# Normalising attention probabilities on VectorE in the place of GpSimd: a hybrid Mamba-2 and attention layer in f32 on Trainium2

## The chip, the cores and the metric

One core of one Trainium2 chip runs the whole layer as one launch. The metric is the device time of that launch in microseconds, the median of the runs shown. The text names the engines as the profile does: PE is TensorE's matmuls (PEld its weight loads), DVE is VectorE, ACT is ScalarE, POOL is GpSimd, SP issues the DMAs.

## What is computed

The layer norms its input (adaLN), projects it, feeds two mixers (a Mamba-2 branch and a causal attention with a forget bias), merges them through gates, projects again, adds the residual and norms once more. The change lies in the attention: sequence 1024, 8 heads of 128.

```python
def one_block(args):                      # one block of 128 queries
    qi, fi, pi = args
    logits = jnp.einsum("bhqd,bhkd->bhqk", qi, k).astype(jnp.float32) * scale
    logits = logits + fi[..., :, None] - f_cum[..., None, :]
    logits = jnp.where(pi[:, None] >= kpos[None, :], logits, -jnp.inf)
    probs = jax.nn.softmax(logits, axis=-1).astype(v.dtype)
    return jnp.einsum("bhqk,bhkd->bhqd", probs, v)
...
o = lax.map(one_block, (qb, fq, qpos))
return o * jax.nn.silu(z)
```

Everything is f32. The kernel splits each f32 operand of a product into a high and a low part (names ending in h and l) and sums three matmuls.

## The kernel before

The kernel first projects, then runs the Mamba-2 branch, then the attention (about 728 to 1020 us of the profiled execution), then the merge and the output products. `attend(h, ...)` treats one head. Its 1024 queries are taken as four pairs of 128-query blocks, the longest first (qq = 3, 2, 1, 0); a block b sees n = (b + 1) x 128 keys, so rows have 128 to 1024 columns. For each block:

- L1028, POOL: a triangular mask is put into the forget bias `fb` (128x128).
- L1036, PE: logits into the PSUM tile `lg` (two buffers of 512 columns), three matmuls each.
- L1037, DVE: logits plus bias go to the SBUF tile `pr`, with the row's minimum into `sm` (the logits are negated); L1041, DVE, combines two minima where n is over 512.
- L1042, ACT: the exponential in place, with the row's sum into `sm`; L1044, DVE: its reciprocal.
- L1045, POOL: `pr` times the reciprocal times 0.5, in place. This is the normalisation.

Then for the pair of blocks: L1057, PE, transposes 128x128 pieces of `pr` into the PSUM tile `tp` (two buffers); L1060, ACT, copies them as the high part `pth`, and L1061, DVE, makes the low part `ptl`; L1067, PE, multiplies with v into `pv` (one PSUM buffer); L1070, DVE, multiplies `pv` with the gate `zg`, which also frees `pv` for the next pair.

Other work lies between these steps. The q and k of the next head are projected on PE at L111 to L113 (some are loaded from memory instead), v is loaded for two heads at a time (`v_load`: DMA into `vt`, L98 ACT cast to `vh`, L99 DVE subtraction to `vl`), `u_scaled` (L812 to L815) loads, scales on DVE and stores pieces of the Mamba branch, and behind heads 6 and 7 `early` runs some of the merge's products (L919 to L921, operands `bh` and `bl` made by L98 and L99). `vt`, `ut` and `zg` share one pool of four buffers.

The order within each engine's queue is not the order of the code. The kernel is built with a scheduler that plays through a timeline of its own and appends each instruction to its engine's queue, attention first (`high_priority`); buffers and semaphores follow from it. So an operation that is put on another engine changes the order on all of them from there on. DMAs are issued by SP.

Of the kernel before, what the change touches and what calls it, by code (L numbers as in the profile page):

```python
# [65 lines left out]
def build(ctx, tc, t):  # L66
    nc = tc.nc
    V, A, G, PE, SP = nc.vector, nc.scalar, nc.gpsimd, nc.tensor, nc.sync
# [7 lines left out]
    def f32(ap):  # L76
        return ap.bitcast(F32)
# [559 lines left out]
    with tc.tile_pool(name="sd", bufs=1, side="right") as sd, \  # L637
# [152 lines left out]
        for tb in range(8):  # L790
# [4 lines left out]
                        scalar1=1.0 / 1024, scalar2=4 * EPS, op0=ALU.mult, op1=ALU.add)  # L795
# [184 lines left out]
    with tc.tile_pool(name="at", bufs=1, side="right") as at, \  # L980
# [36 lines left out]
        def attend(h, q, vhl, zg):  # L1017
            qh, ql, kh, kl = q
            vh, vl = vhl
            vs = slice((h % 2) * P, (h % 2 + 1) * P)  # L1020
            fb = at.tile([P, S], F32, tag="fb", bufs=2, name="fb")
            SP.dma_start(out=fb, in_=f_scr[8 * h:8 * h + 8].rearrange("(o c) l -> o (c l)", o=1).broadcast_to([P, S]))
            for qq in (3, 2, 1, 0):
                prs = {}
                for b in (2 * qq + 1, 2 * qq):
                    n = (b + 1) * P
                    bs = slice(b * P, n)
                    G.affine_select(out=fb[:, bs], in_=fb[:, bs], pattern=[[-1, P]], channel_multiplier=1, base=0,  # L1028
                                    compare_op=ALU.is_ge, fill=BIG)
                    pr = at.tile([P, S], F32, tag="pr", bufs=4, name="pr")  # L1030
                    sm = at.tile([P, 2], F32, tag="sm", bufs=4, name="sm")
                    for n0 in range(0, n, 512):
                        n1 = min(n, n0 + 512)
                        lg = atp.tile([P, 512], F32, tag="lg", bufs=2, name="lg")
                        for i, (x, y) in enumerate(((qh, kh), (qh, kl), (ql, kh))):
                            PE.matmul(lg[:, :n1 - n0], lhsT=x[:, bs], rhs=y[:, n0:n1], start=(i == 0), stop=(i == 2))  # L1036
                        V.tensor_tensor_reduce(out=pr[:, n0:n1], in0=lg[:, :n1 - n0], in1=fb[:, n0:n1], op0=ALU.add,  # L1037
                                               op1=ALU.min, scale=1.0, scalar=BIG,
                                               accum_out=sm[:, n0 // 512:n0 // 512 + 1])
                    if n > 512:  # L1040
                        V.tensor_tensor(out=sm[:, 0:1], in0=sm[:, 0:1], in1=sm[:, 1:2], op=ALU.min)  # L1041
                    A.activation(out=pr[:, :n], in_=pr[:, :n], func=AF.Exp, scale=-1.0, bias=sm[:, 0:1],  # L1042
                                 accum_out=sm[:, 1:2])
                    V.reciprocal(out=sm[:, 1:2], in_=sm[:, 1:2])  # L1044
                    G.tensor_scalar(out=pr[:, :n], in0=pr[:, :n], scalar1=sm[:, 1:2], scalar2=0.5,  # L1045
                                    op0=ALU.mult, op1=ALU.mult)
                    prs[b] = pr
                pv = atp.tile([P, 512], F32, tag="pv", bufs=1, name="pv")
                for jp in range(qq + 1):
                    last = jp == qq  # L1050
                    w = 384 if last else 512
                    tp = atp.tile([P, 512], F32, tag="tp", bufs=2, name="tp")
                    blocks = [(2 * jp, 2 * qq, 0), (2 * jp, 2 * qq + 1, 128)]
                    blocks += [(2 * jp + 1, 2 * qq + 1, 256)] if last else [(2 * jp + 1, 2 * qq, 256),
                                                                           (2 * jp + 1, 2 * qq + 1, 384)]
                    for kb, b, o in blocks:
                        PE.transpose(out=tp[:, o:o + P], in_=prs[b][:, kb * P:(kb + 1) * P], identity=ident)  # L1057
                    pth = at.tile([P, 512], F32R, tag="pth", bufs=2, name="pth")
                    ptl = at.tile([P, 512], F32R, tag="ptl", bufs=2, name="ptl")
                    A.copy(out=pth[:, :w], in_=tp[:, :w])  # L1060
                    V.tensor_tensor(out=ptl[:, :w], in0=tp[:, :w], in1=f32(pth[:, :w]), op=ALU.subtract)  # L1061
                    for kb in (2 * jp, 2 * jp + 1):
                        d = (kb % 2) * 256
                        o0 = 128 if (last and kb % 2) else 0
                        m = 256 - o0
                        for i, (x, y) in enumerate(((vh, pth), (vl, pth), (vh, ptl))):
                            PE.matmul(pv[:, o0:256], lhsT=x[kb // 4][:, kb % 4, vs], rhs=y[:, d:d + m],  # L1067
                                      start=(kb == 0 and i == 0), stop=(kb == 2 * qq + 1 and i == 2))
                o = zg[:, qq * 256:(qq + 1) * 256]
                V.tensor_tensor(out=o, in0=pv[:, :256], in1=o, op=ALU.mult)  # L1070
            SP.dma_start(out=o_scr[h], in_=zg[:, :S])
# [6 lines left out]
        for h in range(AH):  # L1078
            if h == HCLOSE:
                hctx.close()  # L1080
                fin = finx.enter_context(tc.tile_pool(name="fin", bufs=1))
            zg = z_load(h)
            with tc.high_priority(offset=APRI):
                attend(h, qkt, vv, zg)
            if h < AH - 1:
                if h % 2:
                    vv = v_load((h + 1) // 2)
                qkt = qk_slab(h + 1)
            if h in EARLY:
                early(EARLY[h])  # L1090
                if 1 in EARLY[h]:
                    ub = b_quads(us_scr, (12, 22))
            for _ in range(PREP[h]):
                u_scaled(next(prep))
# [158 lines left out]
```

## Time and profile before

| | us |
|---|---|
| median of 3 runs | 1218.62 (1217.94 to 1220.36) |
| the profiled execution | 1224.31 |
| its span in the trace | 1222.6 |
| PE busy | 1165.0 (95%) |
| DVE busy | 955.9 (78%) |
| ACT busy | 635.5 (52%) |
| POOL busy | 88.4 (7%) |

The profile is of one execution, whose time stands beside its span: what the trace shows is measured against 1222.6, not against the median. PE's granted clock over the span was 0.988 of full speed. Busy shares are averages over stages; the stage of the change is 292 us long.

### The profile page before, as it was taken

The numbers are of one execution on the slowest core, as the hardware profiler recorded it, in microseconds if no ns is written. First come the engines' busy times: TensorE is split into PE (matmuls) and PEld (weight loads), VectorE is DVE, ScalarE is ACT, GpSimd is POOL, SyncE is SP. The second block draws the span as 40 slices with busy tenths as digits, with TensorE's granted clock in tenths as the row PEclk, the third lists the DMA queues.
The fourth block names the chain that finished last, engine by engine and source line by source line (L and its number), as shares of the span: only waits on it lengthen the run. The fifth ranks groups of instructions, "written<-read, shape, count | busy, mean of one in ns | idle before, by whom it ended". The sixth has DMA issues, their size and how long they took to land.

```text
span 1222.6 us, 18382 instructions
## 1 busy us (share of the span) xinstructions
PE 1165.0 (95%) x6206; PEld 981.2 (80%) x6206; DVE 955.9 (78%) x1946; ACT 635.5 (52%) x1260; POOL 88.4 (7%) x152
## 2 busy tenths in 40 slices
PE   3999999999999999999999989999988999999997
PEld 2788888788877877998887778888877887788876
DVE  5856699788987784589999986664677977989967
ACT  7554443454443334776676633454456554454465
POOL 1000000000000000000000012222322220000001
PEclk9999999999999999999999989999998999999999
DMA  9665643655485676546545668422246526875334
GB/s 370 263 243 166 218 138 100 207 204 176 156 290 171 218 239 201 186 152 222 186 154 178 207 216 286 144 94 81 87 165 203 175 88 228 283 241 181 109 95 147
DMA packets 109018, 228.26 MB, mean 187 GB/s; under 512 B 12362, under 2 KB 20220, under 8 KB 107900
## 3 DMA queue, kind: packets, MB, share of 16 engines
q1 hardware_dynamic: 108924, 227.09, 55.2%
q8 instruction: 49, 0.80, 0.3%
q14 instruction: 45, 0.37, 0.1%
HBM read 159.14 MB, written 67.90 MB: 186 GB/s over the span
## 4 chain that ended last, share of the span: by engine, by line
PE 62%; DVE 16%; DMA 13%; ACT 4%; issue 4%; SPq 1%; POOL 0%; POOLq 0%; DVEq 0%; ACTq 0%
PE pp L497 4%; PE pv L1067 4%; PE pp L499 4%; PE pp L500 4%; PE lg L1036 3%; PE mm L497 3%; PE mm L499 3%; PE mm L500 3%; PE mm L112 3%; PE mm L113 3%; PE mm L111 3%; PE tp L1057 2%; DMA ab<-a_scr 2%; DMA wr<-w_c 2%; PE mm L919 2%
## 5 line engine op out<-in xcount | busy, mean ns | idle before, releaser
L98 ACT CAST wh<-wr 128x512 fp32r<-128x512 f32 (+1 forms) x214 | 131.0, 620 | 176.2 <-DMA wr<-w_c 32.4
L99 DVE TENSOR_TENSOR wl<-wr,wh 128x512 fp32r<-128x512 f32 (+1 forms) x214 | 146.9, 693 | 44.0 <-ACT wh L98 43.3
L112 PE MATMUL mm<-hl,wh 128*128 128x512 f32 x288 | 116.7, 405 | 0.4 <-DVE hl L306 0.4
L111 PE MATMUL mm<-hh,wh 128*128 128x512 f32 x288 | 116.2, 408 | 0.0
L113 PE MATMUL mm<-hh,wl 128*128 128x512 f32 x288 | 115.5, 402 | 0.0
L136 PE MATMUL mm<-wh,hh 128*128 128x256 f32 (+1 forms) x256 | 73.7, 289 | 1.9 <-DVE tmp L348 1.9
L137 PE MATMUL mm<-wl,hh 128*128 128x256 f32 (+1 forms) x256 | 74.4, 291 | 0.0
L138 PE MATMUL mm<-wh,hl 128*128 128x256 f32 (+1 forms) x256 | 73.7, 289 | 0.0
L1042 ACT ACTIVATE pr<-pr,sm 128x1024 f32<-128x1024 f32 (+3 forms) x64 | 49.9, 780 | 42.4 <-DVE sm L1041 35.1
L1060 ACT CAST pth<-tp 128x512 fp32r<-128x512 f32 (+1 forms) x80 | 42.4, 543 | 47.7 <-PE tp L1057 39.5
L1037 DVE CUSTOM_DVE_ANT_0 pr<-lg,fb 128x512 f32<-128x512 f32 (+1 forms) x96 | 51.4, 552 | 17.0 <-PE lg L1036 12.4
L112 PEld LDWEIGHTS mm<-hl,wh 128*128 128x128 f32 x288 | 55.2, 192 | 11.0 <-DVE hl L306 1.0
L113 PEld LDWEIGHTS mm<-hh,wl 128*128 128x128 f32 x288 | 55.0, 191 | 10.4
L111 PEld LDWEIGHTS mm<-hh,wh 128*128 128x128 f32 x288 | 54.7, 193 | 10.2 <-ACT hh L305 0.3
L690 ACT ACTIVATE ab<-ab,acs 128x128 f32<-128x128 f32 x128 | 41.2, 391 | 40.7 <-DMA ab<-a_scr 40.5
L1045 POOL TENSOR_SCALAR pr<-pr,sm 128x1024 f32<-128x1024 f32 (+3 forms) x64 | 51.8, 811 | 87.5 <-DVE sm L1044 70.2
L1061 DVE TENSOR_TENSOR ptl<-tp,pth 128x512 fp32r<-128x512 f32 (+1 forms) x80 | 50.0, 632 | 10.3 <-ACT pth L1060 10.2
L98 ACT CAST sh<-sr 128x512 fp32r<-128x512 f32 x57 | 34.0, 619 | 43.8 <-DVE sr L479 32.4
L796 POOL TENSOR_TENSOR fl<-fl,mhalf 128x8 f32<-128x8 f32 x1 | 1.6, 1647 | 698.2 <-DVE fl L794 698.2
L136 PEld LDWEIGHTS mm<-wh,hh 128*128 128x128 f32 x256 | 48.8, 191 | 2.4 <-DVE tmp L348 2.2
L1067 PE MATMUL pv<-pth,vh 128*128 128x256 f32 (+1 forms) x160 | 45.8, 287 | 4.5 <-DVE zg L1070 3.8
L138 PEld LDWEIGHTS mm<-wh,hl 128*128 128x128 f32 x256 | 49.1, 192 | 0.0
(407 smaller groups left out, 3509.8 us busy)
## 6 DMA issues: line engine op xcount, KB each, us to landing
wr<-w_c SPq DMA_DIRECT2D x116, 256.0 KB, 3.9
wa<-w_ada SPq DMA_DIRECT2D x8, 1024.0 KB, 11.4
g_scr<-gt SPq DMA_DIRECT2D x16, 512.0 KB, 4.2
ab<-a_scr SPq DMA_DIRECT2D x32, 256.0 KB, 3.9
gt<-g_scr SPq DMA_DIRECT2D x32, 256.0 KB, 3.7
wr<-w_ps SPq DMA_DIRECT2D x28, 256.0 KB, 2.6
wr<-w_pa SPq DMA_DIRECT2D x28, 256.0 KB, 2.8
wr<-so SPq DMA_DIRECT2D x28, 256.0 KB, 2.7
```

The lines of the kernel that those rows point to most:

```text
L98: A.copy(out=hi[:, :n], in_=raw[:, :n])
L99: eng.tensor_tensor(out=lo[:, :n], in0=raw[:, :n], in1=f32(hi[:, :n]), op=ALU.subtract)
L111: PE.matmul(ps, lhsT=hi[:, cs], rhs=xh[k][:, hs], start=(k == 0), stop=False)
L112: PE.matmul(ps, lhsT=hi[:, cs], rhs=xl[k][:, hs], start=False, stop=False)
L113: PE.matmul(ps, lhsT=lo[:, cs], rhs=xh[k][:, hs], start=False, stop=(k == 7))
L136: PE.matmul(o, lhsT=xh[k][:, ts], rhs=hi[:, cs], start=(k == 0), stop=False)
L137: PE.matmul(o, lhsT=xh[k][:, ts], rhs=lo[:, cs], start=False, stop=False)
L138: PE.matmul(o, lhsT=xl[k][:, ts], rhs=hi[:, cs], start=False, stop=(k == 7))
L497: PE.matmul(ps, lhsT=f[0][:, w], rhs=xh[:, hs], start=(first and k == 0), stop=False, skip_group_check=True)
L499: PE.matmul(ps, lhsT=f[0][:, w], rhs=xl[:, hs], start=False, stop=False, skip_group_check=True)
L500: PE.matmul(ps, lhsT=f[1][:, w], rhs=xh[:, hs], start=False, stop=(k == 3), skip_group_check=True)
L1067: PE.matmul(pv[:, o0:256], lhsT=x[kb // 4][:, kb % 4, vs], rhs=y[:, d:d + m], start=(kb == 0 and i == 0), stop=(kb == 2 * qq + 1 and i == 2))
```

## The change

One line: the normalisation L1045 is issued on VectorE instead of GpSimd, with the same operands.

```diff
@@ -1042,7 +1042,7 @@
                     A.activation(out=pr[:, :n], in_=pr[:, :n], func=AF.Exp, scale=-1.0, bias=sm[:, 0:1],
                                  accum_out=sm[:, 1:2])
                     V.reciprocal(out=sm[:, 1:2], in_=sm[:, 1:2])
-                    G.tensor_scalar(out=pr[:, :n], in0=pr[:, :n], scalar1=sm[:, 1:2], scalar2=0.5,
+                    V.tensor_scalar(out=pr[:, :n], in0=pr[:, :n], scalar1=sm[:, 1:2], scalar2=0.5,
                                     op0=ALU.mult, op1=ALU.mult)
                     prs[b] = pr
```

These are 64 instructions (8 heads of 8 blocks). All other instructions stay; the scheduler sets the queues of PE, DVE and ACT anew from the first head on. Three places of the order:

Head 0, ACT, while the values of the next pair of heads are loaded; before:

```order
L1060 CAST pth<-tp 128x384
L1042 ACTIVATE pr,sm<-pr,sm 128x512
L98 CAST vh<-vt 128x1024
L1042 ACTIVATE pr,sm<-pr,sm 128x384
L1060 CAST pth<-tp 128x512 x2
```

and with the change:

```order
L1060 CAST pth<-tp 128x384
L98 CAST vh<-vt 128x1024
L1042 ACTIVATE pr,sm<-pr,sm 128x512
L1042 ACTIVATE pr,sm<-pr,sm 128x384
L1060 CAST pth<-tp 128x512 x2
```

The cast of `vh`, which waits for a DMA, has moved ahead of the exponential of 512 columns. The same place on DVE, before:

```order
L1037 ISA pr,sm<-lg,fb 128x384
L1037 ISA sm 128x1
L1044 RECIPROCAL sm<-sm 128x1
L99 TENSOR_TENSOR vl<-vt,vh 128x1024
L1044 RECIPROCAL sm<-sm 128x1
L1070 TENSOR_TENSOR zg<-pv,zg 128x256
L1061 TENSOR_TENSOR ptl<-tp,pth 128x512 x2
```

and with the change:

```order
L1037 ISA pr,sm<-lg,fb 128x384
L1037 ISA sm 128x1
L99 TENSOR_TENSOR vl<-vt,vh 128x1024
L1044 RECIPROCAL sm<-sm 128x1 x2
L1045 TENSOR_SCALAR pr<-pr,sm 128x512
L1045 TENSOR_SCALAR pr<-pr,sm 128x384
L1061 TENSOR_TENSOR ptl<-tp,pth 128x512
L1070 TENSOR_TENSOR zg<-pv,zg 128x256
L1037 ISA pr,sm<-lg,fb 128x256
```

Both normalisations and one `ptl` now stand ahead of `zg`, and `vl` ahead of both reciprocals.

Head 6, DVE, where `early` forms its operands; before:

```order
L99 TENSOR_TENSOR bl<-wr,bh 128x512
L1070 TENSOR_TENSOR zg<-pv,zg 128x256
L99 TENSOR_TENSOR bl<-wr,bh 128x512
L1041 TENSOR_TENSOR sm<-sm 128x1
L1037 ISA pr,sm<-lg,fb 128x512
L1037 ISA sm 128x1
L1037 ISA pr,sm<-lg,fb 128x128
L1037 ISA sm 128x1
```

and with the change:

```order
L99 TENSOR_TENSOR bl<-wr,bh 128x512
L1045 TENSOR_SCALAR pr<-pr,sm 128x1024
L1070 TENSOR_TENSOR zg<-pv,zg 128x256
L99 TENSOR_TENSOR bl<-wr,bh 128x512
L1041 TENSOR_TENSOR sm<-sm 128x1
L1037 ISA pr,sm<-lg,fb 128x512
L1037 ISA sm 128x1
L1044 RECIPROCAL sm<-sm 128x1
L1037 ISA pr,sm<-lg,fb 128x128
L1037 ISA sm 128x1
```

A normalisation of 1024 columns stands between the first `bl` and `zg`, and a reciprocal before the last eviction.

Head 7, DVE, the last long blocks; before:

```order
L1044 RECIPROCAL sm<-sm 128x1
L1041 TENSOR_TENSOR sm<-sm 128x1
L1037 ISA pr,sm<-lg,fb 128x512
L1037 ISA sm 128x1
L1037 ISA pr,sm<-lg,fb 128x128
L1037 ISA sm 128x1
L1044 RECIPROCAL sm<-sm 128x1
L1041 TENSOR_TENSOR sm<-sm 128x1
L1044 RECIPROCAL sm<-sm 128x1
```

and with the change:

```order
L1041 TENSOR_TENSOR sm<-sm 128x1
L1037 ISA pr,sm<-lg,fb 128x512
L1037 ISA sm 128x1
L1044 RECIPROCAL sm<-sm 128x1
L1037 ISA pr,sm<-lg,fb 128x128
L1037 ISA sm 128x1
L1045 TENSOR_SCALAR pr<-pr,sm 128x896
L1041 TENSOR_TENSOR sm<-sm 128x1
L1044 RECIPROCAL sm<-sm 128x1
L1045 TENSOR_SCALAR pr<-pr,sm 128x768
```

The reciprocal of the 896-column block has moved behind the eviction of 512 columns, and its normalisation behind that of 128. PE at the same place, as a difference (minus is before, plus with the change):

```order
 L1036 MATMUL lg<-kh,ql 128x128
-L1057 MATMUL tp<-ident,pr 128x128 x8
 L1036 MATMUL lg<-kh,qh 128x512
 L1036 MATMUL lg<-kl,qh 128x512
 L1036 MATMUL lg<-kh,ql 128x512
 L1036 MATMUL lg<-kh,qh 128x384
 L1036 MATMUL lg<-kl,qh 128x384
 L1036 MATMUL lg<-kh,ql 128x384
+L1057 MATMUL tp<-ident,pr 128x128 x8
 L1067 MATMUL pv<-pth,vh 128x256
```

The eight transposes of the first pair have moved behind six logit matmuls of the next.

## Rows read from the trace of the kernel before

**Rows 1.** The page: busy us of each engine (share of the span) and instructions, and the shares of the chain that ended last.
```profile
PE 1165.0 (95%) x6206; PEld 981.2 (80%) x6206; DVE 955.9 (78%) x1946; ACT 635.5 (52%) x1260; POOL 88.4 (7%) x152
...
PE 62%; DVE 16%; DMA 13%; ACT 4%; issue 4%; SPq 1%; POOL 0%; POOLq 0%; DVEq 0%; ACTq 0%
```

**Rows 2.** Windows: the attention stage and its dense middle; columns: stretch, us, then busy us (instructions) of PE, PEld, DVE, ACT and POOL, granted PE clock, DMA share, GB/s.
```profile
728.00:1020.00 292.00, 279.90 (x1599) 242.78 (x1600) 200.50 (x513) 145.57 (x294) 76.31 (x128) 0.97 0.44 145
775.00:900.00 125.00, 123.84 (x755) 109.50 (x754) 76.89 (x221) 60.49 (x124) 35.28 (x63) 1.00 0.30 101
```

**Rows 3.** PE's waits in 728 to 1020 us: us in total, times, longest us.
```profile
PE lg L1036 <- DVE sm L1037: 5.0, 5, 3.2
PE pv L1067 <- DVE zg L1070: 3.8, 4, 2.2
PE lg L1036 <- DMA fb<-f_scr: 1.5, 1, 1.5
...
PE tp L1057 <- POOL pr L1045: 0.5, 1, 0.5
```

**Rows 4.** The page's costliest groups: the normalisation; busy us, mean ns of one, idle us before it.
```profile
L1045 POOL TENSOR_SCALAR pr<-pr,sm 128x1024 f32<-128x1024 f32 (+3 forms) x64 | 51.8, 811 | 87.5 <-DVE sm L1044 70.2
```

**Rows 5.** Timeline of the tail, all engines (start us, us, engine, line, operation, out<-in, count, and in brackets the idle time before it and what ended it).
```profile
1000.95 1.00 POOL L1045 TENSOR_SCALAR pr<-pr,sm 128x896 f32<-128x896 f32 x1
...
1002.00 1.09 PE L1057 MATMUL tp<-ident,pr 128*128 128x128 f32 x8 [0.46 <-POOL pr L1045]
...
1010.37 1.48 DVE L1061 TENSOR_TENSOR ptl<-tp,pth 128x512 fp32r<-128x512 f32 x2
...
1011.10 0.19 PEld L1067 LDWEIGHTS pv<-ptl,vh 128*128 128x128 f32 x1 [0.24 <-DVE ptl L1061]
```

**Rows 6.** Timeline, all engines, at two places where a normalisation runs beside DVE.
```profile
739.52 2.61 POOL L1045 TENSOR_SCALAR pr<-pr,sm 128x1024 f32<-128x1024 f32 x1 [6.27 <-DVE sm L1044]
...
739.92 1.28 DVE L813 SCALAR_TENSOR_TENSOR ut<-ut,cols,rb 128x1024 f32<-128x1024 f32 x1
...
913.18 1.12 POOL L1045 TENSOR_SCALAR pr<-pr,sm 128x1024 f32<-128x1024 f32 x1 [0.89 <-DVE sm L1044]
...
913.52 0.78 DVE L1041 TENSOR_TENSOR sm<-sm 128x1 f32<-128x1 f32 x1
```

**Rows 7.** Groups of DVE by shape: three of the whole span, and L813 in 728 to 1020 us: busy us, mean ns of one | idle us before.
```profile
L543 DVE TENSOR_SCALAR cv<-xp,cols 128x1024 f32<-128x1024 f32 x10 | 7.7, 808 | 0.2 <-ACT xp L539 0.2
...
L285 DVE TENSOR_SCALAR acc<-wa,cols 128x256 f32<-128x256 f32 x8 | 2.8, 347 | 1.1 <-DMA wa<-w_ada 1.1
...
L560 DVE TENSOR_SCALAR gb<-wga,cols 128x1024 f32<-128x1024 f32 x1 | 0.8, 758 | 0.0
...
L813 DVE SCALAR_TENSOR_TENSOR ut<-ut,cols,rb 128x1024 f32<-128x1024 f32 x8 | 10.2, 1284 | 10.2 <-DMA ut<-u_scr 6.6 <-DMA rb<-r_scr 3.6
```

**Rows 8.** Timeline of ACT, head 0.
```profile
762.10 0.72 ACT L1042 ACTIVATE pr<-pr,sm 128x512 f32<-128x512 f32 x1 [0.98 <-DVE sm L1037]
...
764.08 1.04 ACT L98 CAST vh<-vt 128x1024 fp32r<-128x1024 f32 x1 [1.17 <-DMA vt<-v_scr]
765.03 0.61 ACT L1042 ACTIVATE pr<-pr,sm 128x384 f32<-128x384 f32 x1
```

**Rows 9.** Timeline of DVE, head 0.
```profile
765.16 1.23 DVE L99 TENSOR_TENSOR vl<-vt,vh 128x1024 fp32r<-128x1024 f32 x1 [2.05 <-ACT vh L98]
766.30 0.15 DVE L1044 RECIPROCAL sm<-sm 128x1 f32<-128x1 f32 x1
766.38 0.41 DVE L1070 TENSOR_TENSOR zg<-pv,zg 128x256 f32<-128x256 f32 x1
766.70 1.28 DVE L1061 TENSOR_TENSOR ptl<-tp,pth 128x512 fp32r<-128x512 f32 x2
```

**Rows 10.** Timeline of PE, head 0.
```profile
766.93 0.36 PE L1067 MATMUL pv<-pth,vh 128*128 128x256 f32 x1 [2.23 <-DVE zg L1070]
```

**Rows 11.** Windows behind the two longest gaps of PE in the stage (columns as in rows 2).
```profile
767.70:771.00 3.30, 3.30 (x18) 3.30 (x17) 1.90 (x5) 0.88 (x1) 0.29 (x1) 0.50 0.37 144
771.10:775.00 3.90, 3.90 (x19) 3.17 (x19) 3.19 (x8) 2.56 (x8) 1.05 (x2) 1.00 0.39 99
...
918.50:924.60 6.10, 6.10 (x21) 5.23 (x22) 4.46 (x12) 4.96 (x10) 3.25 (x4) 0.50 0.90 311
```

**Rows 12.** Timeline at head 6, all engines.
```profile
914.97 0.62 ACT L98 CAST bh<-wr 128x512 fp32r<-128x512 f32 x1 [3.43 <-DMA wr<-us_scr]
914.98 0.28 PE L1036 MATMUL lg<-kh,ql 128*128 128x128 f32 x1
915.62 0.69 DVE L99 TENSOR_TENSOR bl<-wr,bh 128x512 fp32r<-128x512 f32 x1 [0.97 <-ACT bh L98]
916.23 0.42 DVE L1070 TENSOR_TENSOR zg<-pv,zg 128x256 f32<-128x256 f32 x1
...
916.99 0.69 DVE L99 TENSOR_TENSOR bl<-wr,bh 128x512 fp32r<-128x512 f32 x1 [0.34 <-ACT bh L98]
917.59 0.15 DVE L1041 TENSOR_TENSOR sm<-sm 128x1 f32<-128x1 f32 x1
917.66 0.69 DVE L1037 CUSTOM_DVE_ANT_0 pr<-lg,fb 128x512 f32<-128x512 f32 x1
...
918.41 0.80 PE L1036 MATMUL lg<-kh,qh 128*128 128x512 f32 x1 [3.15 <-DVE sm L1037]
```


## Prediction

> **What bounds the kernel now.** I read the busy line of the page first: PE is busy 95% of the span, DVE 78%, ACT 52%, POOL 7%, and the chain that ended last lies on PE for 62% and on POOL for 0% [rows 1]. TensorE sets the time. The change touches only the attention, so next comes that stage alone, 728 to 1020 us: PE is busy 279.9 of 292.0 us, so it idles 12.1; DVE is busy 200.5, POOL 76.3 [rows 2]. What PE waits for there is the next view: 5.0 us for DVE to evict logits, 3.8 for DVE's zg, 1.5 for a DMA, and 0.5, once, for the normalised probabilities of POOL [rows 3]. The reader is to see that GpSimd's lateness costs 0.5 us and VectorE's close to 9: the change moves work off an engine that nobody waits for, onto the one that PE waits for most. In the dense middle, 775 to 900, PE loses only 1.2 of 125 us and DVE has 48 us free [rows 2]. What happens is therefore decided at a few places.
>
> **What is removed.** POOL's 64 normalisations, 51.8 us busy [rows 4]. PE's one wait for them stands at 1002.00 [rows 5]. The PE queue after the change puts six lg matmuls ahead of these transposes, and their buffer is freed by an eviction that ends near 1002, so the idle time there hardly goes. I take -0.3, bounds 0 and -0.5.
>
> The normalisation itself gets shorter: an undisturbed 1024-column one takes 1.12 us on POOL [rows 6] and, by the price below, 0.76 on DVE; over all 64 that is 51.8 against 33.2, or 18.6 us of latency. By the waits only 0.5 of it is latency that PE sees. The Trainium skill (GPSIMD Engine Reference, section 4.1, Engine selection) says that elementwise work on a tile belongs on VectorE, GpSimd being roughly at line rate with one input and about 2x slower with two. By the rows and the price the factor is 1.5. By the rule the sum would be a gain, up to 18.6 us if all of that latency counted, and by the waits no more than 0.5 us.
>
> **What is added.** 64 TENSOR_SCALARs of 128 to 1024 columns on DVE, eight of each size. The trace has no such operation with a per-partition pointer and a constant. The nearest rows are f32 TENSOR_SCALARs from SBUF to SBUF: 758 ns at 1024 columns, 347 at 256, and 808 for a form with two pointers [rows 7]. The line through the first two is 210 ns + 0.535 per column: 0.76, 0.69, 0.62, 0.55, 0.48, 0.42, 0.35, 0.28 from 1024 down to 128, together 4.15 us a head and 33.2 for eight heads. With the 50 ns of a second pointer it is 36.4; at the price of a two-tensor operation (1284 ns at 1024 [rows 7]), 33.2 x 1.69 = 56. I take 33.2 to 36, since the operation has one tensor. DVE in the stage goes from 69% to 81% and still has 56 us free, so the sum of the work decides nothing. What hides it are DVE's gaps, in which it waits for ACT's exponentials and PE's logits, and PE's filler (the next head's q and k products). Where the order puts a normalisation directly ahead of something that PE takes at once, the cover is gone and its whole length is paid.
>
> **Place A, head 0, the largest term.** Before, the exponential of 512 columns runs on ACT at 762.10, and only then ACT waits, 1.17 us, for the load of v: vh runs at 764.08, the exponential of 384 at 765.03 [rows 8]. DVE's vl starts at 765.16, the second reciprocal at 766.30, zg at 766.38 [rows 9], and PE, idle 2.23 us, starts pv at 766.93 [rows 10]. After, the vh cast stands ahead of both exponentials, and DVE has vl, two reciprocals, two normalisations (512, 384), one ptl and only then zg. My working, with the trace's durations: vh to 765.13, the exponentials (pipelined steps of 0.72 and 0.61) to 766.46; vl to 766.39, reciprocals to 766.7, normalisations +0.48 +0.42, to 767.6; ptl (0.64, half of the two at 766.70 [rows 9]) to 768.2; zg to 768.5; pv at about 768.6, +1.7. Three transposes that came behind the pv now run inside the wait, -0.3 (eight take 1.09 us [rows 5]). **+1.4**; bounds +0.3 (the load lands early or ACT is ready sooner) and +1.7.
>
> The gap also touches the clock. After the idle 2.23 us, PE ran at a granted clock of 0.5 from 767.7 to 771.0, 3.3 us, and at 1.0 again from 771.1; after the idle 3.15 us before 918.41 it ran at 0.5 for 6.1 us, to 924.6 [rows 11, 12]. Those are the 1.2 and the 2.4 GHz level. The new gap is 3.6 to 3.9 us with three transposes in it, so nearer to the second. Another 3 us or so at half speed costs 1.5 to 1.7: bounds 0 and +1.7, taken **+1.2**.
>
> **Place B, head 6.** PE stands from 915.26 to 918.41 because its next lg waits for the eviction at 917.66, behind bl, zg, bl and a combine of minima on DVE [rows 12]. After, a 1024-column normalisation stands between the first bl and zg: 0.76 more. DVE had 0.34 idle before the second bl [rows 12], which absorbs that much: **+0.4**, bounds 0 and 0.76.
>
> **The tail, head 7, without filler.** The 896-column normalisation now stands behind the evictions of 512 and 128 columns. It ends about 1003.1 instead of 1001.95 [rows 5]; that is 1.15 later, and the six lg matmuls moved ahead cover most of it: +0.3. At 1010.37 ptl is started as soon as zg is done and PE waits for it until 1011.10 [rows 5]; a 384-column normalisation now stands ahead: +0.4. The last transposes moved behind a pv: +0.2. Together **+0.9**, bounds 0 and 1.5.
>
> **Elsewhere.** In six other places of heads 1, 3, 4 and 5 a normalisation stands directly ahead of a zg, ptl or eviction that PE uses soon: three of 512, one each of 640, 384 and 1024 columns, 3.2 us by the price. The order of PE's queue has been redone around them, and the dense stretch loses only 1.2 in 125 us now [rows 2], so I take under a third, **+0.9**, bounds 0 and 3.2.
>
> **Sum:** -0.3 + 1.4 + 1.2 + 0.4 + 0.9 + 0.9 = **+4.5 us**. It is made against the profiled execution (1224.31 us, span 1222.6), which ran 5.7 above the median; the stage's waits should be the same in the others, so the sum is put on the median, 1218.62: **1223.1 us**. About 0.2%, 2.4 us, is what a measurement of this kernel tells from no change: the three runs shown spread by 2.4. The sum of the bounds is -0.2 to +8.9.
>
> **Rivals.**
> - *Hidden.* All of it falls in DVE's gaps. For: 56 us still free, dense stretch without PE waits. Against: places A, B and the tail are exactly where DVE is last. It needs the load at A to land by about 762, before the exponentials are ready; then A and its clock fall away (-2.6) and the rest, +1.9, is below what can be told: 1220.5.
> - *Faster.* POOL and DVE hold each other now: a 1024-column normalisation took 2.61 us at 739.52 while L813 ran beside it, and a one-element combine took 0.78 at 913.52, under a normalisation, instead of the 0.15 at 917.59 [rows 6, 12]. Without POOL reading, DVE's results come earlier. If that closes the 3.15 us gap before 918.41, it and half of the 6.1 us at half clock go, -6.2; with the other terms at half (+2) the time is 1214.4. It decides if the first bl, at 915.62 now, can start some 3 us earlier. Against: after the held combine DVE waits 0.97 us for ACT's bh cast at 914.97 anyway [rows 12], so the lead is thrown away there. The Trainium skill (SBUF — State Buffer, Who interferes with whom) says that GpSimd shares DVE's second port pair, and that a DVE instruction with two SBUF inputs and a GpSimd one that reads SBUF block each other, whichever starts first winning; the trace agrees at both rows.
> - *Slower by much.* The operation costs nearer 1284 ns at 1024 (56 us in all, DVE at 88%), all places pay in full (8.9) and two or three gaps more grow long enough to draw a stretch at half clock of 3.3 us each, 1.65 lost: +12, 1230.6. For: PE takes many DVE results at once. Against: the price rows.
>
> **How the numbers follow.** Forecast (+2.4 to +8) 0.43; much slower (+8 to +13) 0.12; hidden (within 2.4) 0.28; faster (-2.4 to -7) 0.17. So slower 0.55, same 0.28, faster 0.17. The range leaves out the lower half of the faster case (0.08) and the upper part of the slow one (0.06): 1214 to 1230; that of the forecast by itself is 1221 to 1226.6.
>
> **What would show it.** Right: L1045 on DVE at about 0.76 us for 1024 columns and 33 to 36 us in all; DVE near 235 us in the stage; PE's wait for zg at head 0 up from 2.2 to over 3.5, with a half-clock stretch of 5 to 7 us behind it; the gap of 3.15 slightly longer. The stage then lasts some 4 us more, and what follows it as long as before. Wrong: the vt load landing earlier, the vh cast off ACT's path, the gap at head 6 gone, or L1045 above 1 us at 1024 columns, each of which would move the sum by more than its own term, since a gap takes its half-clock stretch with it.

## The result, and the profile after

The changed kernel takes 1225.62 us (median of 5 runs, 1223.99 to 1226.98) against 1220.19 for the kernel before (5 runs): the ratio is 1.0044, 95% interval 1.0027 to 1.0060, 5.4 us slower. The forecast was 1223.1, 4.5 us slower than the 1218.62 it started from.

The two profiled executions do not show this in their spans, 1222.3 us after and 1222.6 before: the profiled execution of before (1224.31) ran 4 us above its median, that of after (1223.99) 1.6 below. So the spans say nothing here, and the reading goes place by place (times in a trace are microseconds from the start of its own span). The page of after, busy time of each engine and the shares of the chain (compare [rows 1]):

```profile
PE 1163.0 (95%) x6206; PEld 979.3 (80%) x6206; DVE 981.6 (80%) x2010; ACT 634.4 (52%) x1260; POOL 38.3 (3%) x88
...
PE 64%; DVE 13%; DMA 13%; ACT 4%; issue 4%; SPq 1%; POOL 0%; DVEq 0%; POOLq 0%; ACTq 0%
```

POOL has lost 50 us, DVE has gained 25.7, and the chain still lies on PE. The attention stage, in the columns of [rows 2]:

```profile
728.00:1020.00 292.00, 277.56 (x1594) 240.69 (x1592) 225.00 (x576) 144.03 (x293) 25.52 (x63) 0.98 0.43 144
...
775.00:900.00 125.00, 123.82 (x754) 109.56 (x753) 90.43 (x250) 61.04 (x125) 12.95 (x31) 1.00 0.28 95
```

DVE goes from 200.5 to 225.0 us, less than the 33 added; the dense middle loses 1.2 us of PE in both kernels. PE's waits in the stage, in the form of [rows 3]:

```profile
PE lg L1036 <- DVE sm L1037: 4.9, 6, 2.7
PE tp L1057 <- DVE ptl L1061: 3.1, 1, 3.1
PE pv L1067 <- DVE zg L1070: 3.1, 2, 2.7
PE pv L1067 <- DVE ptl L1061: 1.0, 4, 0.4
...
PE pv L1067 <- DVE sm L1044: 0.7, 1, 0.7
```

The wait for POOL is gone, and all that is shown here is for DVE (left out: 0.9 for ACT's pth). A new kind stands second: transposes that wait 3.1 us for a ptl. That is head 0 (PE's and DVE's timeline, and ACT's behind it):

```profile
766.20 0.55 PE L1057 MATMUL tp<-ident,pr 128*128 128x128 f32 x3 [3.09 <-DVE ptl L1061]
766.62 0.36 PE L1067 MATMUL pv<-pth,vh 128*128 128x256 f32 x1
```
```profile
764.50 0.34 DVE L1044 RECIPROCAL sm<-sm 128x1 f32<-128x1 f32 x2
764.75 0.80 DVE L1045 TENSOR_SCALAR pr<-pr,sm 128x512 f32<-128x512 f32 x2
765.46 0.68 DVE L1061 TENSOR_TENSOR ptl<-tp,pth 128x512 fp32r<-128x512 f32 x1
766.06 0.41 DVE L1070 TENSOR_TENSOR zg<-pv,zg 128x256 f32<-128x256 f32 x1
```
```profile
762.28 1.05 ACT L98 CAST vh<-vt 128x1024 fp32r<-128x1024 f32 x1 [2.67 <-DMA vt<-v_scr]
763.23 0.72 ACT L1042 ACTIVATE pr<-pr,sm 128x512 f32<-128x512 f32 x1
...
763.95 0.60 ACT L1042 ACTIVATE pr<-pr,sm 128x384 f32<-128x384 f32 x1
```

The vh cast runs first, both exponentials behind it, and DVE does two reciprocals, two normalisations (0.80 us for the two) and a ptl before zg, as the order said. PE idles 3.09 us, against 2.23 in [rows 10]. From the start of the vh cast to the end of PE's wait it is 3.92 us here (762.28 to 766.20) and 2.85 before (764.08 [rows 8] to 766.93 [rows 10]); the experiments come back to these two numbers.

The normalisation on DVE, by size, the combine of minima and the low parts of early's operands, in groups of the stage (busy us, mean ns of one):

```profile
L99 DVE TENSOR_TENSOR bl<-wr,bh 128x512 fp32r<-128x512 f32 x16 | 10.7, 686 | 1.7 <-ACT bh L98 1.6
...
L1045 DVE TENSOR_SCALAR pr<-pr,sm 128x1024 f32<-128x1024 f32 x8 | 6.0, 752 | 0.2
...
L1041 DVE TENSOR_TENSOR sm<-sm 128x1 f32<-128x1 f32 x32 | 4.9, 152 | 0.2
...
L1045 DVE TENSOR_SCALAR pr<-pr,sm 128x128 f32<-128x128 f32 x8 | 2.3, 283 | 0.1
```
```profile
L1045 DVE TENSOR_SCALAR pr<-pr,sm 128x1024 f32<-128x1024 f32 (+3 forms) x64 | 33.0, 520 | 1.2
```

752 ns at 1024 columns and 283 at 128: the line through [rows 7] gave 758 and 278, and 33.2 us in all. The combine L1041 fell from a mean of 215 ns, the row of before,

```profile
L1041 DVE TENSOR_TENSOR sm<-sm 128x1 f32<-128x1 f32 x32 | 6.9, 215 | 0.1
```

to 152, with no normalisation on POOL beside it any more.

Two further places. The first is the zg of head 5 (DVE, then PE, then the same pv before, which waited 0.59 us):

```profile
932.97 0.48 DVE L1045 TENSOR_SCALAR pr<-pr,sm 128x512 f32<-128x512 f32 x1
...
933.44 0.67 DVE L954 TENSOR_TENSOR wr<-b,wr 128x512 f32<-128x512 f32 x1
934.03 0.42 DVE L1070 TENSOR_TENSOR zg<-pv,zg 128x256 f32<-128x256 f32 x1
```
```profile
934.59 0.55 PE L1067 MATMUL pv<-pth,vh 128*128 128x256 f32 x1 [2.66 <-DVE zg L1070]
```
```profile
935.41 0.36 PE L1067 MATMUL pv<-pth,vh 128*128 128x256 f32 x1 [0.59 <-DVE zg L1070]
```

The second is the place that the prediction calls head 6 (its order is that of early's operands, which stand behind head 6 in the code). By the count of zg it lies between head 4's last block and head 5's first. Its normalisation is there, and the gap is 2.74 us where [rows 12] has 3.15:

```profile
914.57 0.75 DVE L1045 TENSOR_SCALAR pr<-pr,sm 128x1024 f32<-128x1024 f32 x1
...
915.73 0.69 DVE L99 TENSOR_TENSOR bl<-wr,bh 128x512 fp32r<-128x512 f32 x1
...
917.16 0.58 PE L1036 MATMUL lg<-kh,qh 128*128 128x512 f32 x1 [2.74 <-DVE sm L1037]
```

The granted clock behind the gap at head 0, and behind that at 934 (columns as in [rows 2]):

```profile
767.20:770.60 3.40, 3.40 (x16) 3.11 (x15) 3.16 (x8) 2.37 (x6) 0.28 (x1) 0.51 0.40 141
770.70:775.00 4.30, 4.30 (x22) 3.52 (x21) 2.42 (x7) 1.21 (x2) 0.30 (x1) 1.00 0.52 155
...
934.60:937.90 3.30, 3.30 (x15) 3.27 (x16) 3.30 (x6) 0.47 (x1) 0.00 (x0) 0.50 0.00 0
```

Both stretches run at 0.5, the 1.2 GHz level, for about 3.4 us; the first is no longer than that of [rows 11], the second is new.

### The profile page after: what moved, and what is told of

It is laid out like the page before. It is cut to its first block, busy times and chain, and to the rows that moved or that the text cites. A ratio compares the mean times of both kernels' runs of the same rounds, so it can differ in the third digit from the quotient of the medians.

```text
span 1222.3 us, 18276 instructions
## 1 busy us (share of the span) xinstructions
PE 1163.0 (95%) x6206; PEld 979.3 (80%) x6206; DVE 981.6 (80%) x2010; ACT 634.4 (52%) x1260; POOL 38.3 (3%) x88
## 4 chain that ended last, share of the span: by engine, by line
PE 64%; DVE 13%; DMA 13%; ACT 4%; issue 4%; SPq 1%; POOL 0%; DVEq 0%; POOLq 0%; ACTq 0%
PE pp L497 4%; PE pp L499 4%; PE pp L500 4%; PE pv L1067 4%; PE mm L112 3%; PE mm L113 3%; PE mm L497 3%; PE mm L111 3%; PE mm L499 3%; PE mm L500 3%; PE lg L1036 3%; DMA ab<-a_scr 2%; PE tp L1057 2%; PE mm L136 1%; PE mm L137 1%
## 5 line engine op out<-in xcount | busy, mean ns | idle before, releaser
L112 PEld LDWEIGHTS mm<-hl,wh 128*128 128x128 f32 x288 | 55.0, 191 | 11.1 <-DVE hl L306 1.0
L1067 PE MATMUL pv<-ptl,vh 128*128 128x256 f32 (+1 forms) x160 | 48.3, 302 | 1.2 <-DVE ptl L1061 1.0
L137 PEld LDWEIGHTS mm<-wl,hh 128*128 128x128 f32 x256 | 48.9, 191 | 0.2
```

Of the source, the lines that this page charges most:

```text
L112: PE.matmul(ps, lhsT=hi[:, cs], rhs=xl[k][:, hs], start=False, stop=False)
L137: PE.matmul(o, lhsT=xh[k][:, ts], rhs=lo[:, cs], start=False, stop=False)
```

## Experiments

**Again, to know what belongs to one execution.** The kernel before and the changed one, unchanged, traced a second and the changed one a third time.

> The kernel before, unchanged, for a second trace of it. It tells which of the traced differences are the program's and which belong to one execution. Few places: the gaps of PE at head 0 (2.23 us), before 918.41 (3.15) and the small ones near 935 (0.59, 0.27, 0.81) come again within 0.3 us. Clock by chance: the stretches at half clock (6.8, 3.4 and 6.8 us long behind 727, 767 and 918) differ in length from one execution to the next, by whole steps of 3.4 us.

> The changed kernel, unchanged, timed once more and traced a second time. Few places: 5 us over before again (0.3 to 0.6%), with the gaps of 3.09 us at head 0 and 2.66 us at 934.6 both there, the second with a stretch at half clock behind it. Clock by chance: the two gaps stay but the stretch at 934 may be missing or twice as long, and the difference to before moves by 1.7 us per step of 3.4 us.

> The changed kernel, unchanged, a third time, beside the two that follow. If the whole is what the first two comparisons gave, 5 to 6 us over before. If the parts by head are right and the whole was read too high by chance, about 2 us over before. In the trace: gap at head 0 over 3 us, gap of 2.4 to 2.7 us near 934, both with a stretch at half clock.

The two further comparisons gave 1.0049 [1.0033, 1.0066] and 1.0040 [1.0020, 1.0060]: the whole is 5 to 6 us, three times. The gaps are the program's, but not to 0.3 us. Kernel before, second trace (PE, head 0 and the place behind head 4):

```profile
772.68 0.36 PE L1067 MATMUL pv<-pth,vh 128*128 128x256 f32 x1 [2.63 <-DVE zg L1070]
```
```profile
924.91 0.80 PE L1036 MATMUL lg<-kh,qh 128*128 128x512 f32 x1 [3.97 <-DVE sm L1037]
```

2.23 became 2.63, 3.15 became 3.97. The stretches at half clock behind 727, 767 and 918 came again with the lengths of the first trace; one of 3.4 us at 1020, which the first trace has, did not. Changed kernel, second and third trace, head 0:

```profile
770.67 0.33 PE L1057 MATMUL tp<-ident,pr 128*128 128x128 f32 x1 [3.36 <-DVE ptl L1061]
```
```profile
764.45 0.47 PE L1057 MATMUL tp<-ident,pr 128*128 128x128 f32 x1 [3.51 <-DVE ptl L1061]
```

The gap at 934 was 2.66, 2.38 and 1.65 us in the three traces, the last less than expected, and half clock followed each. The granted clock, which every timed run lists as a mean, is lower with the change in both comparisons that list it for both kernels: 0.9887 (6 runs) against 0.9909 (17), and 0.9855 (12) against 0.9892 (29). One minus the clock, times the span, is the time that PE loses to it: 13.9 against 11.1 us, and 17.8 against 13.2. So 2.8 us of 6.0 come with the clock in the first comparison, 4.6 of 4.9 in the second, and the rest without.

**The change undone for a head or two.**

```diff
-                    V.tensor_scalar(out=pr[:, :n], in0=pr[:, :n], scalar1=sm[:, 1:2], scalar2=0.5,
+                    (G if h == 0 else V).tensor_scalar(out=pr[:, :n], in0=pr[:, :n], scalar1=sm[:, 1:2], scalar2=0.5,
```

and `h in (4, 5)` in the second.

> The change undone for head 0 alone: its 8 normalisations on POOL, the other 56 on DVE. Few places: the gap at head 0 falls from 3.09 us to the 2.2 of before and the rest stays, so 4 us over before (1.3 less than the changed kernel). Spread evenly over the heads: one eighth of 5.4 us comes back, 4.7 us over before. In the trace the exponential of 512 columns stands ahead of the vh cast again.

> The change undone for heads 4 and 5: 16 normalisations on POOL, 48 on DVE. Few places: the gap of 2.66 us at 934.6 shrinks to the 0.6 of before and its stretch at half clock (1.7 us) goes, 3.8 us less than the changed kernel, so 1.6 us over before (0.13%). Spread evenly over the heads: a quarter of 5.4 us comes back, 4 us over before.

Measured: 1.0042 [1.0026, 1.0059] and 1.0035 [1.0019, 1.0051] over before, beside 1.0049 for the changed kernel on the same chip: 5.1 and 4.3 us. For the first, 4 and 4.7 both lie in the interval; for the second (2.3 to 6.2 us) the 1.6 of few places does not, the 4 of an even spread does. The gaps did what was expected. PE at head 0 in the first, and another wait that had not been foreseen, 11 us earlier:

```profile
768.98 0.36 PE L1067 MATMUL pv<-pth,vh 128*128 128x256 f32 x1 [2.02 <-DVE zg L1070]
```
```profile
757.83 0.39 PE L1067 MATMUL pv<-ptl,vh 128*128 128x256 f32 x1 [1.08 <-DVE ptl L1061]
```

and PE at head 5 in the second:

```profile
935.30 0.36 PE L1067 MATMUL pv<-pth,vh 128*128 128x256 f32 x1 [0.67 <-DVE zg L1070]
```

0.67 instead of 2.66, and no half clock there; yet the time fell by 1.7 us only, which the intervals do not tell from nothing. The account by place below says why: what the gap at 934 costs had come back at the place before it.

**One group of heads on DVE alone.** The condition is turned round (`V if h == 0 else G`, then heads 1 to 3, 4 and 5, 6 and 7). From the end of such a group on the order is that of before.

> Only head 0 normalised on DVE, heads 1 to 7 on POOL; from head 1 on the order is that of before. Few places: the gap of head 0 is the 3.1 to 3.4 us of the changed kernel, 1.3 us lost, and the stretch at half clock behind it comes in more executions than before, another 0 to 1.7: 1.3 to 3 us over before. Spread evenly: 0.7 us.

> Only heads 1 to 3 on DVE, where the normalisation has the filler of the next head's q and k beside it. Few places: no gap of PE over 0.3 us beside those of before, within 1 us of before. Spread evenly: three eighths of 5.4, 2 us over before.

> Only heads 4 and 5 on DVE. Few places: the gap of 2.4 to 2.7 us before the pv near 934 with its stretch at half clock, 2.1 + 1.7 = 3.8 us over before. Spread evenly: 1.4 us.

> Only heads 6 and 7 on DVE, the tail among them. Few places: the tail's gaps of the changed kernel, 0.7 us more idle than before, so 0 to 1 us over before. Spread evenly: 1.4 us. The four runs of this set add up to the change if the parts do not touch each other: 5.4 us.

| on DVE | ratio to before | 95% interval |
|---|---|---|
| head 0 | 1.0010 | 0.9995 to 1.0025 |
| heads 1 to 3 | 0.9994 | 0.9976 to 1.0012 |
| heads 4, 5 | 1.0003 | 0.9982 to 1.0024 |
| heads 6, 7 | 1.0009 | 0.9989 to 1.0029 |

Together 0.16%, 2 us, with an interval of some 4.5 us to either side (the root of the summed squares of the four half widths, times 1220): this neither adds up to the change nor contradicts it. 3.8 us for heads 4 and 5 is outside (0.24% is 2.9), and so are the 2 us of an even spread for heads 1 to 3 (0.12% is 1.5). By time alone no group stands out. In the trace of heads 4 and 5 the expected gap near 934 did not come: that pv waits 0.9 us for zg and no half clock follows, so heads 4 and 5 by themselves do not make the gap of 1.65 to 2.66 us there.

**What the traces say, place by place.** With the groups there are eleven traces that share PE instructions. Head 0 first: in six of them head 0 has the order of before, in five that of the change. PE's gap before the pv (or, with the change, before the transposes ahead of it), and whether a stretch of half clock of about 3.4 us follows:

| head 0 as before | gap, us | half clock | head 0 as changed | gap, us | half clock |
|---|---|---|---|---|---|
| before | 2.23 | yes | changed | 3.09 | yes |
| before, second | 2.63 | yes | changed, second | 3.36 | yes |
| heads 1 to 3 | 2.40 | yes | changed, third | 3.51 | yes |
| head 0 undone | 2.02 | no | heads 4, 5 undone | 3.62 | yes |
| heads 6, 7 | 2.73 | no | head 0 alone | 3.67 | yes |
| heads 4, 5 | 0.38 | no | | | |

The row with the smallest and one with the largest gap:

```profile
766.18 0.36 PE L1067 MATMUL pv<-pth,vh 128*128 128x256 f32 x1 [0.38 <-ACT pth L1060]
```
```profile
770.12 0.33 PE L1057 MATMUL tp<-ident,pr 128*128 128x128 f32 x1 [3.67 <-DVE ptl L1061]
```

And the clock over the 3.5 us from the end of the gap on, in heads 6, 7 (full) and in head 0 alone (half):

```profile
765.80:769.30 3.50, 3.42 (x23) 3.11 (x24) 2.63 (x6) 1.14 (x3) 0.63 (x2) 1.00 0.52 150
```
```profile
770.50:774.00 3.50, 3.50 (x15) 3.20 (x14) 3.40 (x9) 2.42 (x6) 0.29 (x1) 0.51 0.36 110
```

The means are 2.07 and 3.45 us, and the half clock comes in 3 of 6 and in 5 of 5. (With eight such stretches in eleven traces, all five would fall on the changed order by chance about once in eight times.)

How long PE waits depends on when the load of v lands. ACT waits for it in all eleven traces, also in that with 0.38 us:

```profile
763.34 1.05 ACT L98 CAST vh<-vt 128x1024 fp32r<-128x1024 f32 x1 [1.42 <-DMA vt<-v_scr]
```

There the cast starts 0.74 us earlier than in the first trace of before and PE comes to the place 1.1 us later, so before the change the place could also cost next to nothing. What does not scatter is the chain behind the load. From the start of the vh cast to the end of PE's wait it takes 2.84 or 2.85 us in each of the six traces with the order of before, and 3.92 or 3.93 in each of the five with that of the change. The order adds 1.08 us, every time; the rest of the difference between the two means is the load's.

To see what arrives on the path, I took the start of the same PE instructions in a trace and in the first trace of before, and how the difference grows across a stretch in which both have the same work to do (first the traces of the unchanged programs, then those of the variants):

| stretch | traces with its order changed | traces with its order of before |
|---|---|---|
| head 0 (736 to 800) | +1.5, +1.8, +0.8, +0.8, +2.4 | 0, +0.4, +0.1, +0.2, -0.2, -3.4 |
| heads 1 to 3 (800 to 900) | +0.3, +0.2, +0.2, +0.5, +0.3, +0.4 | 0, +0.1, 0, -0.2, +0.1 |
| heads 4, 5 (900 to 970) | +0.2, +0.1, +1.3, +0.4, +1.0 | 0, +0.4, -0.3, +0.1, -0.2, -0.7 |
| heads 6, 7 (970 to 1027) | +1.4, +1.4, +1.3, +1.4, +1.1, +1.1 | 0, +0.2, 0, +0.2, 0 |

The last line leaves out a stretch of half clock at 1020 (3.4 us, 1.7 lost) where only one of the two has it. By the difference of the means the change costs 1.9 us at head 0 (1.4 without the trace with the 0.38 us gap), 0.3 at heads 1 to 3, 0.7 at heads 4 and 5, 1.2 in the tail: 4.1 in all. That the gap at 934 weighs little is seen in the third line: every trace with the order of before has half clock for over 6 us behind the gap near 918, two of the three of the changed kernel for 3.4, and another 3.4 behind 934.

**The load of v taken out of the way.** In both kernels the scaling of the Mamba pieces is spread, so that the load for heads 2 and 3 is not queued behind their buffers at head 0.

```diff
-PREP = (6, 1, 0, 0, 0, 0, 0, 0, 1)
+PREP = (2, 1, 2, 2, 0, 0, 0, 0, 1)
```

> The changed kernel with the scaling of the Mamba pieces spread: PREP = (2, 1, 2, 2, ...) in the place of (6, 1, 0, 0, ...), so four pieces that were scaled in head 0 come in heads 2 and 3, and the load of v for heads 2 and 3 no longer waits behind their stores. Few places: the gap at head 0 (3.1 to 3.4 us with a stretch at half clock) goes to under 0.5, 4 us or more less than the changed kernel, so about before or a little under. Spread evenly: only the DMA wait goes, with the same gain in both kernels, 2.2 to 3.9 us.

> The same spreading in the kernel before. Few places: the gap of 2.2 to 2.6 us at head 0 and its stretch at half clock go, 2 to 4 us less than before; the normalisation on DVE then costs only what the place near 934 costs, so spread_u_dve is 2.5 to 4 us slower than this one. Spread evenly: spread_u_dve is 5.4 us slower than this one, as with the wait.

Measured: 0.9985 [0.9968, 1.0002] with the normalisation on DVE, 0.9983 [0.9963, 1.0002] with it on POOL. Neither can be told from before, and between the two lie 0.02%, 0.2 us, with some 3 us of uncertainty. PE has no gap at head 0 in either trace (ACT still waits 2.7 and 3.3 us for a load of v, at 746 and 748, while PE has other work). PE's waits, first with DVE, then with POOL:

```profile
PE lg L1036 <- DVE sm L1037: 6.1, 5, 3.9
PE tp L1057 <- DVE ptl L1061: 1.6, 1, 1.6
PE pv L1067 <- DVE zg L1070: 1.3, 3, 0.6
...
PE tp L1057 <- DVE pr L1045: 0.3, 1, 0.3
```
```profile
PE lg L1036 <- DVE sm L1037: 6.0, 6, 3.6
PE pv L1067 <- DVE zg L1070: 1.5, 3, 0.6
...
PE tp L1057 <- POOL pr L1045: 0.5, 1, 0.5
```

The 5.4 us of an even spread lie outside; of the 2.5 to 4 of few places only the lower end is inside. With DVE the transposes near 931 still wait 1.6 us for a ptl, without half clock behind them. The scheduler sets another order in the tail too, and from 900 to 1045 both traces gain the same against before, 2.1 us. The mean granted clock is 0.9905 with DVE and 0.9904 with POOL, so the change takes nothing from the clock here. The 33 us on DVE stayed and cost nothing that can be told, so the loss is no price of DVE's time as such: it hangs on the wait for v and on the order that the scheduler makes around it. Which of these two it is more was not parted, since the edit changes both.

**POOL's free time used.** The low parts of the early products, made on POOL.

```diff
-                fs.append(b_split(e))
+                fs.append(b_split(e, G))
```

> spread_u_dve with the low parts bl of the early products (20 subtractions of 128x512) made on POOL, which the change has left idle, in the place of DVE. Few places: at the two places of heads 4 and 5 DVE no longer stands behind bl's wait for a DMA, so the gap of 3.2 us before the lg near 918 and that of 2.7 near 934 shrink, with their half clock: 3 to 8 us less than spread_u_dve, and under before. Against: POOL's masks of the forget bias stand behind bl in its queue and the gap stays, 0.

Measured: 1214.75 us (median of 6) against 1221.5 (of 29), a ratio of 0.9930 [0.9904, 0.9957]: 8.5 us faster than before by the ratio, 6.8 by the medians, and the fastest kernel here. (There are twelve such subtractions, not twenty.) PE's wait for evictions, the subtraction on POOL, and the window behind 914.8 us (columns as in [rows 2]):

```profile
PE lg L1036 <- DVE sm L1037: 4.1, 7, 0.9
```
```profile
L99 POOL TENSOR_TENSOR bl<-wr,bh 128x512 fp32r<-128x512 f32 x12 | 16.0, 1354 | 6.4 <-ACT bh L98 5.3 <-DMA wr<-us_scr 0.9
```
```profile
914.80:918.00 3.20, 3.20 (x12) 2.64 (x13) 1.02 (x8) 2.84 (x6) 1.65 (x3) 0.50 1.04 407
```

The longest wait falls from 3.9 us to 0.9, although a subtraction takes 1354 ns on POOL against 686 on DVE: DVE's queue no longer stands behind operands that a DMA brings late. From 900 to 1027 us this trace gains 6.2 us on that of the variant it starts from. The half clock that was expected to go with the gap stayed: 3.4 us, as in the other two traces with the scaling spread, here behind waits of 0.28, 0.56 and 0.86 us. It was not run in the kernel before, with POOL also normalising.

## Why the prediction was right

**The bound and the removed wait.** Right. The one wait for POOL (0.46 us at 1002.00 [rows 5]) is now a wait of the same length for an eviction, the one that the prediction named:

```profile
1001.45 0.50 PE L1036 MATMUL lg<-kh,qh 128*128 128x512 f32 x1 [0.46 <-DVE sm L1037]
...
1001.59 0.68 DVE L1045 TENSOR_SCALAR pr<-pr,sm 128x896 f32<-128x896 f32 x1
...
1002.78 1.04 PE L1057 MATMUL tp<-ident,pr 128*128 128x128 f32 x8
```

so the gain was 0, not 0.3.

**The price.** Right: 33.0 us in all against 33.2 to 36. DVE's busy time in the stage is 225 us and not 235. The forecast added durations, and busy time counts a moment once, while records of consecutive DVE instructions overlap: the normalisations of 764.75 start before the reciprocals of 764.50 (0.34 us) have ended. Over the whole span the 64 normalisations add 28 us that no other record fills. The rest of DVE's work fills 2.3 us less than before, of which L1041, with no normalisation on POOL beside it, is 2.0.

**Head 0.** Right in mechanism. The gap was put at 3.6 to 3.9 us and is 3.1 to 3.7; the loss by idling was put at 1.4. The means (3.45 less 2.07) give the same, by luck: the chain behind the load grew by 1.08 in every trace, and the rest is the one trace with the early load. Of the chain, the two normalisations took 0.80 for the 0.90 of the working, and the three transposes that now run ahead of the pv 0.4 to 0.6 for its 0.3. The clock was wrong in kind: the prediction let the stretch double behind a longer gap (+1.2). It did not; it came each time instead of in half of the traces, which is 0.85 (half of 1.7) if that is no chance. The two make 1.9, as the account by place measured, against 2.6.

**The place behind head 4 (called head 6).** Wrong, and small: +0.4 was forecast, and the gap is 2.74, 3.18 and 3.94 us with the change, 3.15 and 3.97 without. The ready time of bh, by a DMA, still sets it in the first trace: from the start of the second bh cast to the end of the gap it is 2.08 us with the change and 2.07 before.

**The tail.** Right in kind, a little small: 1.2 us against 0.9. Transposes stand behind six lg matmuls and start at 1002.78 for 1002.00, and PE's idle time from 971 to 1018 is 3.8 us for 3.1. So 0.7 of the 1.2 is idle time; where the rest lies was not shown.

**Elsewhere.** Forecast +0.9 without clock. Heads 1 to 3 give 0.3, and the gap at 934, which the prediction had not named by its time, some 0.7 with the place before it: 1.0 for the 1.3 of both terms.

**Sum.** 4.1 us by the places, 4.5 forecast, 5.4 measured, with an interval of 3.3 to 7.3 us. That the sum came so near is in part luck: head 0 was put 0.7 too high, the tail 0.3 too low, and the places leave 1.3 us of the measured loss unexplained, though within its noise. Of the rivals, *faster* fell where the prediction said it would: L1041 is no longer held and the gap stayed. *Hidden* came true only in the variant that takes the load of v away, under the condition that the prediction gave for it. The rule that elementwise work belongs on VectorE (the Trainium skill, GPSIMD Engine Reference, section 4.1) holds for the instruction: 752 ns against 1.12 us, and for two inputs 686 against 1354. It did not hold for the kernel.

What stays open: about half of the measured loss in one comparison and nearly all of it in the other comes with a lower mean clock of the timed runs. The traces hold one stretch more with the change (934) and one that comes each time (head 0), but longer ones without it (behind 918), so that the time lost to half clock from the first logit to 1045 us is 6.7, 6.8 and 11.6 us in the three traces with the change and 9.7 and 8.0 in the two without. Where the untraced runs lose it was not shown. Nor was an order of before with the normalisation on DVE, which would part engine and order for good: the scheduler sets both at once.

## What to carry to other kernels

Moving work from an idle engine to one that others wait for was decided here by a few places where that engine's results are awaited without cover; they show in the waits, not in the busy shares. Where a scheduler orders the queues, a moved instruction moves its neighbours, and the same 33 us cost 5 us in one arrangement and nothing that could be told in another. The largest gain of this set came from giving the idle engine work that made a busy queue wait for a DMA, though it ran twice as long there; that is one variant of one kernel.

## What was not expected of the hardware

A gap of PE at the same place is not the same length in each execution: 0.38 to 2.73 us with one order, by when one load lands, while the chain behind the load was 2.84 or 2.85 us in all six traces. Gaps of 2.02 and 2.73 us were followed by full clock, of 2.23, 2.40 and 2.63 by 3.4 us at the 1.2 GHz level, and every one from 3.09 to 3.67 by such a stretch. Behind the gap near 918 the stretch was 3.4 us in two of the eleven traces and over 6 in the others; with the scaling spread it was 3.4 in all three, also where PE's longest wait ahead of it was 0.9 us. A subtraction with two SBUF inputs took 1354 ns on POOL, 1.97 times the 686 on DVE, and a one-input normalisation of 1024 columns 1.5 times.
